# Latent attention as one sequence of steps, and row maxima turned four columns at once

## The chip, the core and the metric

The kernel runs on one core of one Trainium2 chip. Times are microseconds of device time of that core for one execution; smaller is better. A core has five engines that run their own instruction lists in order and meet through semaphores: TensorE (PE in the profile, with its weight loads as PEld), VectorE (DVE), ScalarE (ACT), GpSimd (POOL), and SyncE (SP), which here issues all DMAs. TensorE writes only to PSUM, which has eight banks of 512 fp32 columns by 128 partitions.

## The reference

One decoder layer over 2048 positions of width 1024. A norm and one input projection feed two groups of heads; their gated outputs go through one output projection, a gated per-layer embedding and a final norm. The change touches the second group only, eight latent heads with 96-wide queries and keys (64 made from a latent, 32 rotary and shared) and 64-wide values, under a causal mask:

```python
def mla_attention(q_nope, q_rope, k_nope, k_rope, v):
    scale = (MLA_NOPE + MLA_ROPE) ** -0.5
    sc = (einsum('bqhd,bkhd->bhqk', qn, k_nope) + einsum('bqhr,bkr->bhqk', qr, k_rope)) * scale
    pr = causal_probs(sc, start, s)          # softmax over the keys up to the query
    return einsum('bhqk,bkhd->bqhd', pr.astype(v.dtype), v)
```

## The kernel before

Four stages follow one another: projections, latent attention, differential attention, output. The latent stage works in *pairs of heads* `pr` (0 to 3) and *tiles of 512 queries* `t` (0 to 3). One head of a pair, `e`, in one tile is called a *run* here; the 32 runs come in the order pr, t, e and are numbered 0 to 31, and the two runs of one pr and t are called a *pair of runs*. A run has n = 4(t+1) steps, one for each block of 128 keys, up to the diagonal; on the last four the query columns left of the diagonal are left out, so they are 512, 384, 256 and 128 wide.

A step has two halves. `scores` makes 128 keys by 512 queries in PSUM with three matmuls of split numbers (lines 583 to 585, and 587 for the mask on the diagonal), exponentiates twice on ACT (588 rounded to `ph`, 589 in full), takes the rest `pl` on DVE (590), and adds `ph` to `acc` on POOL (596, 599) for most steps. The PSUM tile `pst` of a step is held from line 583 to line 590. `av`, three steps later (LAG), multiplies both parts with the values into `po` and `po2` (613, 614, and 616 where TensorE adds the softmax sum). A run ends with `finish`: line 620 adds the column sums of `acc` into `po2`, ACT and DVE put the output together in `ot` (622 to 624), four transposes turn it into `pz` (627), DVE divides (629, 631) and SP stores (633).

Each pair of runs needs a preparation, `prep`: queries and keys (lines 505 to 518), values for even pairs (533 to 535), and for each run the row maxima. `rmax` multiplies 128 queries with 512 keys (547, 549 on the diagonal) and DVE reduces them to a column (550). `row` then gathers the maxima of 512 queries in four columns `m4`, turns them with four transposes into one row of 512 in PSUM (560), and ACT writes the negative of it as row 96 of the queries `QH` (561). The first matmul of `scores` uses 97 rows, the 97th being this one, so a run's first score waits for its row.

PSUM tiles of the latent stage: `ps_m` (2 banks) for all preparation, `ps_s` (4 banks) for `pst`, `ps_o` for `po` and for `po2`, which `pz` shares.

The order is planned in Python. `main` holds the steps of all runs with a cost in TensorE and DVE time, `side` the preparation with its costs. Going backwards through `main`, the planner places side work as late as an even load of DVE allows (RHO, SLACK), and at least MARGIN = 13 entries of `main` ahead of the run that needs it; then the recorded instructions are ordered once more by a list scheduler that has its own estimate of durations and fills waits with whatever is ready. So the order on each engine isn't the order of the code. Before, `main` has each run's steps, its last three `av` alone, and its `finish`, before the next run begins:

```python
            for e in range(2):
                for kc in range(n + LAG):
                    if kc < n:
                        tasks[e].append((0.65 * w, 0.6 * w, lambda e=e, kc=kc: scores(e, kc)))
                    if kc >= LAG:
                        tasks[e].append((0.43 * w, 0, lambda e=e, kc=kc: av(e, kc - LAG)))
                tasks[e].append((1.2, 1.7, lambda e=e: finish(e)))
```

Of the kernel before, what the change touches and what calls it, by code (L numbers as in the profile page):

```python
# [7 lines left out]
F32 = mybir.dt.float32  # L8
# [9 lines left out]
P = 128  # L18
# [13 lines left out]
MARGIN = 13  # attention steps by which a latent head's preparation runs ahead  # L32
RHO = 0.95  # share of the tensor engine's time in which the vector engine may be busy
SLACK = 0.8  # vector work that may pile up
QB = 2  # buffers for a latent head's queries
HE = 6  # steps over which a differential head's loads are spread
WN = 6  # pieces of the output weights loaded in a step
PES = 4  # key blocks whose softmax sums are added by the tensor engine: those with
PEL = (3,)  # kc % PES in PEL
TAIL = 2  # in the last latent step, every TAIL-th of the other sums goes to the vector engine  # L40


def merge(a, b):
    """Runs two lists of (cost, function) side by side, each in its order."""
# [15 lines left out]
def tile_hymba(ctx, tc, a, out):  # L60
# [48 lines left out]
    with ExitStack() as c1:  # L109
# [136 lines left out]
        # gates of the differential heads  # L246
# [23 lines left out]
        # rotary q and k of the differential heads, transposed  # L270
# [28 lines left out]
        # shared rotary key and first gates of the latent heads  # L299
# [31 lines left out]
        # latents and the rotary part of the latent heads' q  # L331
# [100 lines left out]
    def load_head(h):  # L432
        """Queries, keys and values of a differential head, a tile for every 512 positions."""
# [21 lines left out]
    SC_M = 96.0 ** -0.5  # L455
    with ExitStack() as c2:
# [3 lines left out]
        ps_s = c2.enter_context(tc.tile_pool(name="p2pss", bufs=4, space=PSUM, reuse_waits="tile"))  # L460
# [35 lines left out]
        def prep(pr, t):  # L496
            """Keys, queries, values and row maxima of a pair of heads for one tile of 512 positions."""
# [43 lines left out]
            def rmax(e, j, c):  # L541
# [5 lines left out]
                T.matmul(pm[:, :w], lhsT=q, rhs=keys_of(pr, e, c)[0][0:96, :w], start=True, stop=(c < t))  # L547
# [473 lines left out]
```

## Time and profile before

| | us |
|---|---|
| median of 3 runs | 2062.68 (2057.31 to 2063.65) |
| span of the profiled execution | 2063.1 |
| latent stage within it | about 614 to 1199 |
| TensorE busy | 1958.6 (95%) |
| VectorE busy | 1268.7 (61%) |
| ScalarE busy | 934.4 (45%) |
| GpSimd busy | 465.7 (23%) |
| mean granted TensorE clock | 0.986 |

The profiled execution's time is its span, with nothing recorded around it. Shares of busy time are averages over stages with different limits. A matmul's recorded duration overlaps that of the next one, so what one costs is read from the distance between two starts. From the rows of the latent stage a reader should take, pair by pair, how long it lasted and how much of that TensorE and VectorE had work for.

### The profile page before, as it was taken

The page shows a single profiled execution, that of the slowest core. Times are in us where ns is not written, and L with a number is a line of the kernel's source. Part 1 is how long each engine was busy: PE and PEld are TensorE (multiplying, and loading weights), DVE is VectorE, ACT ScalarE, POOL GpSimd, SP SyncE. Part 2 cuts the span into 40 slices and gives each one's busy share as a digit, 9 for nine tenths or more (in the row PEclk, how much of TensorE's full clock was granted, in tenths as well). Part 3 has the DMA queues.
Part 4 walks back from the last instruction along what each step waited for, and adds up shares of the span by engine and source line. Part 5 has one row for each costly group of instructions (what it writes and reads, how often), then busy time and mean ns, then how long its engine had stood idle before and what let it go on. Part 6 is the DMA issues. An engine that isn't in the chain of part 4 may idle for free.

```text
span 2063.1 us, 28013 instructions
## 1 busy us (share of the span) xinstructions
PE 1958.6 (95%) x9793; PEld 1532.6 (74%) x9793; DVE 1268.7 (61%) x2714; ACT 934.4 (45%) x2105; POOL 465.7 (23%) x428
## 2 busy tenths in 40 slices
PE   8999999999989999999999988998898899999997
PEld 5788878898866776766767766776676677777786
DVE  5253676522457878878878887778888533333332
ACT  5422001123336675766666776778687321111111
POOL 4400445200002453534534410000001201111000
PEclk9999999999999999999999999999999999999999
DMA  5442333322120000000032240433011622222210
GB/s 166 136 155 96 124 131 123 113 86 71 42 75 14 16 11 21 14 16 16 11 90 78 59 118 9 128 105 90 6 57 57 230 77 87 87 87 84 78 46 21
DMA packets 126861, 156.20 MB, mean 76 GB/s; under 512 B 30385, under 2 KB 74305, under 8 KB 126721
## 3 DMA queue, kind: packets, MB, share of 16 engines
q1 hardware_dynamic: 126720, 154.42, 24.1%
q8 instruction: 77, 1.26, 0.3%
q14 instruction: 64, 0.52, 0.1%
HBM read 101.41 MB, written 52.96 MB: 75 GB/s over the span
## 4 chain that ended last, share of the span: by engine, by line
PE 75%; DVE 9%; ACT 7%; DMA 2%; issue 2%; POOL 1%; SPq 0%; ACTq 0%; POOLq 0%; DVEq 0%
PE p L914 6%; PE p L916 6%; PE p L915 6%; PE ps L165 5%; PE ps L166 5%; PE ps L164 5%; PE pm L547 3%; PE pod L815 3%; PE pst L583 3%; PE pst L584 3%; PE pst L585 3%; PE po L613 3%; PE po L614 3%; PE ps L284 3%; PE ps L283 3%; PE ps L282 3%
## 5 line engine op out<-in xcount | busy, mean ns | idle before, releaser
L599 POOL TENSOR_TENSOR acc<-ph,acc 128x512 f32<-128x512 f32 (+3 forms) x208 | 218.9, 1052 | 248.1 <-ACT ph L588 161.1
L164 PE MATMUL ps<-wh,xh 128*128 128x512 f32 (+1 forms) x640 | 229.2, 359 | 9.8 <-DVE wh L153 8.4
L165 PE MATMUL ps<-wl,xh 128*128 128x512 f32 (+1 forms) x640 | 227.3, 356 | 0.5 <-DVE wl L154 0.4
L166 PE MATMUL ps<-wh,xl 128*128 128x512 f32 (+1 forms) x640 | 226.3, 356 | 0.3 <-DVE xl L141 0.2
L588 ACT ACTIVATE ph<-pst 128x512 fp32r<-128x512 f32 (+1 forms) x320 | 170.8, 534 | 110.8 <-PE pst L585 66.5
L550 DVE TENSOR_REDUCE mx<-pm 128x1 f32<-128x512 f32 (+2 forms) x320 | 186.6, 605 | 28.6 <-PE pm L547 15.9
L590 DVE TENSOR_TENSOR pl<-pst,ph 128x512 fp32r<-128x512 f32 (+1 forms) x320 | 189.5, 604 | 22.8 <-ACT pst L589 21.2
L751 DVE TENSOR_REDUCE mxd<-pu 128x1 f32<-128x1024 f32 (+4 forms) x192 | 172.8, 909 | 22.7 <-PE pu L750 14.5
L99 POOL TENSOR_TENSOR s<-s,half 128x2 f32<-128x2 f32 (+1 forms) x48 | 32.1, 669 | 649.5 <-DVE s L98 549.6
L762 ACT ACTIVATE pb<-pu,nm 128x1024 f32<-128x1024 f32 (+4 forms) x192 | 165.4, 867 | 24.0 <-DVE nm L757 16.0
L589 ACT ACTIVATE pst<-pst 128x512 f32<-128x512 f32 (+1 forms) x320 | 170.1, 532 | 0.3
L747 PE MATMUL pu<-hd 128*128 128x512 f32 (+3 forms) x320 | 140.7, 440 | 20.4 <-ACT pb L762 19.3
L164 PEld LDWEIGHTS ps<-wh,xh 128*128 128x128 f32 x640 | 121.2, 190 | 29.9 <-ACT sq L136 6.5
L815 PE MATMUL pod<-ah,hd 128*128 128x256 f32 (+1 forms) x576 | 141.8, 371 | 0.5 <-ACT ah L807 0.5
L166 PEld LDWEIGHTS ps<-wh,xl 128*128 128x128 f32 x640 | 121.0, 189 | 19.4 <-DVE xl L141 2.2
L165 PEld LDWEIGHTS ps<-wl,xh 128*128 128x128 f32 x640 | 121.3, 190 | 18.7 <-DVE wl L154 1.9
L963 DVE TENSOR_TENSOR sg<-p,sg 128x512 f32<-128x512 f32 (+1 forms) x34 | 20.8, 655 | 171.5 <-ACT sg L962 171.5
L748 PE MATMUL pu<-hd 128*128 128x512 f32 (+3 forms) x320 | 122.1, 387 | 0.0
L547 PE MATMUL pm<-kall,QH 96*128 96x512 f32 (+3 forms) x288 | 112.2, 403 | 6.9 <-DVE kall L103 4.8
L613 PE MATMUL po<-ph,vall 128*128 128x512 f32 (+1 forms) x320 | 117.1, 394 | 0.5 <-ACT ph L588 0.2
L614 PE MATMUL po<-pl,vall 128*65 128x512 f32 (+1 forms) x320 | 111.9, 371 | 3.7 <-DVE pl L590 2.1
L583 PE MATMUL pst<-QH,kall 97*128 97x512 f32 (+3 forms) x288 | 114.0, 396 | 0.0
(266 smaller groups left out, 4654.1 us busy)
## 6 DMA issues: line engine op xcount, KB each, us to landing
hd<-dq_s SPq DMA_DIRECT2D x192, 128.0 KB, 2.7
wr<-in_w_in SPq DMA_DIRECT2D x40, 256.0 KB, 3.0
xr<-in_xT SPq DMA_DIRECT2D x32, 256.0 KB, 3.7
dq_s<-th SPq DMA_DIRECT2D x32, 256.0 KB, 2.0
dq_s<-tl SPq DMA_DIRECT2D x32, 256.0 KB, 2.0
xr<-in_x SPq DMA_DIRECT2D x16, 512.0 KB, 4.2
gt<-gate_s SPq DMA_DIRECT2D x15, 512.0 KB, 3.4
out<-sg SPq DMA_DIRECT2D x15, 512.0 KB, 2.9
```

What stands on the lines that cost most here:

```text
L164: T.matmul(pt[:, :w], lhsT=h, rhs=wh[k][:, :w], start=(k == 0), stop=False)
L165: T.matmul(pt[:, :w], lhsT=h, rhs=wl[k][:, :w], start=False, stop=False)
L166: T.matmul(pt[:, :w], lhsT=l, rhs=wh[k][:, :w], start=False, stop=(k == KT - 1))
L547: T.matmul(pm[:, :w], lhsT=q, rhs=keys_of(pr, e, c)[0][0:96, :w], start=True, stop=(c < t))
L550: V.reduce_max(box[e][:, j, c:c + 1], pm[:, :w], axis=AX.X)
L583: T.matmul(pt[:, o:], lhsT=kh[0:97], rhs=qh[0:97, o:], start=True, stop=False)
L590: V.tensor_sub(pl[:, o:], pt[:, o:], ph[:, o:].bitcast(F32))
L599: eng.tensor_add(box[e][:, o:], ph[:, o:].bitcast(F32), box[e][:, o:])
L613: T.matmul(po[:, o:], lhsT=vv[:, 0:128], rhs=ph[:, o:], start=(kc == 0), stop=(kc == n - 1))
L614: T.matmul(po2[:65, o:], lhsT=vv[:, 64:129], rhs=pl[:, o:], start=(kc == 0), stop=False)
L751: V.reduce_max(st["x", m][:, u:u + 1], pu[:, :w], axis=AX.X)
L815: T.matmul(st["po"][:, o:], lhsT=vv, rhs=st[u][:, i, o:], start=(kc == 0), stop=(kc == nk - 1))
```

## The change

Line numbers from here on are of the kernel they belong to; after the change scores are lines 593 to 597, `av` 618 to 621, the end of a run 624 to 639, and the turning of the row 558 to 562.

*Rows.* One transpose turns the four columns of `m4` at once into 4 partitions by 128 columns. ACT writes the negative of that into an SBUF tile `mr` (4 by 128), and four DMAs on SP put its four rows into row 96 of `QH`, 512 bytes each (the DMA is cut into 16 pieces of 8 numbers). Where t = 0, `m4` is a view of the maxima and the DVE copy is gone.

*One sequence.* A class `Run` replaces `attend`, and `stream` lists the steps of all 32 runs in one sequence: the first scores of a run stand directly behind the last scores of the run before, and its last three `av` between them. `finish` is cut in two: `gather` after the last `av`, and `store` three steps later. The costs the planner is told are a little higher (0.7 and 0.47 for 0.65 and 0.43; 0.9 and 0.4 on TensorE for 1.2).

*PSUM.* `ps_s` has 3 banks for 4, `po` has 2 for 1, and `pz` takes a bank of `ps_m`, not that of `po2`.

Everything else in the diff removes comments.

```diff
-        ps_s = c2.enter_context(tc.tile_pool(name="p2pss", bufs=4, space=PSUM, reuse_waits="tile"))
+        ps_s = c2.enter_context(tc.tile_pool(name="p2pss", bufs=3, space=PSUM, reuse_waits="tile"))
...
             def row(e):
-                m4 = sb.tile([P, 4], F32, name="m4", tag="m4")
+                m4 = box[e][:, :, 0]
                 if t > 0:
+                    m4 = sb.tile([P, 4], F32, name="m4", tag="m4")
                     V.reduce_max(m4, box[e][:, :, :t + 1], axis=AX.X)
-                else:
-                    V.tensor_copy(m4, box[e][:, :, 0])
-                prow = ps_m.tile([P, 512], F32, name="prow", tag="m")
+                pm = ps_m.tile([P, 512], F32, name="pm4", tag="m")
+                T.transpose(pm[:4, :P], m4, ident)
+                mr = sb.tile([4, P], F32R, name="mr", tag="mr", bufs=4)
+                A.mul(mr, pm[:4, :P], -1.0)
                 for j in range(4):
-                    T.transpose(prow[0:1, j * P:(j + 1) * P], m4[:, j:j + 1], ident)
-                A.mul(QH[pr, t, e][96:97, :], prow[0:1, :], -1.0)
+                    nc.sync.dma_start(out=QH[pr, t, e][96:97, j * P:(j + 1) * P].bitcast(F32),
+                                      in_=mr[j:j + 1, :].bitcast(F32))
...
-                    box["o", e] = (ps_o.tile([P, 512], F32, name="po", tag="po"),
-                                   ps_o.tile([P, 512], F32, name="po2", tag="po2"))
+                    self.po = ps_o.tile([P, 512], F32, name="po", tag="po", bufs=2)
+                    self.po2 = ps_o.tile([P, 512], F32, name="po2", tag="po2")
...
-            def finish(e):
-                po, po2 = box["o", e]
-                T.matmul(po2[:65], lhsT=sel, rhs=box[e], start=False, stop=True)
-                ot = sb.tile([P, 512], F32, name="ot", tag="ot", bufs=1)
...
-                pz = ps_o.tile([P, 4, P], F32, name="pz", tag="po2")
+            def gather(self):
+                T.matmul(self.po2[:65], lhsT=sel, rhs=self.acc, start=False, stop=True)
+                ot = self.ot = sb.tile([P, 512], F32, name="ot", tag="ot", bufs=1)
+                A.copy(ot[:65], self.po2[:65])
+                V.tensor_add(ot[0:64], self.po[0:64], ot[0:64])
+                V.tensor_add(ot[0:64], self.po[64:128], ot[0:64])
+
+            def store(self):
+                pz = ps_m.tile([P, 4, P], F32, name="pz", tag="m")
                 for j in range(4):
-                    T.transpose(pz[:, j, 0:65], ot[0:65, j * P:(j + 1) * P], ident[0:65, 0:65])
+                    T.transpose(pz[:, j, 0:65], self.ot[0:65, j * P:(j + 1) * P], ident[0:65, 0:65])
...
+        def stream(runs):
+            LAG, DROP = 3, 3
+            seq = [(r, kc) for r in runs for kc in range(r.n)]
+            main, start, late = [], [], {}
+            for i in range(len(seq) + LAG + DROP):
+                if i < len(seq):
+                    r, kc = seq[i]
+                    w = 1 - r.where(kc)[2] / 512
+                    if kc == 0:
+                        start.append(len(main))
+                    main.append((0.7 * w, 0.6 * w, lambda r=r, kc=kc: r.scores(kc)))
+                if LAG <= i < len(seq) + LAG:
+                    r, kc = seq[i - LAG]
+                    w = 1 - r.where(kc)[2] / 512
+                    main.append((0.47 * w, 0, lambda r=r, kc=kc: r.av(kc)))
+                    if kc == r.n - 1:
+                        main.append((0.9, 1.4, r.gather))
+                        late[i + DROP] = r
+                if i in late:
+                    main.append((0.4, 0.6, late[i].store))
+            assert len(late) == len(runs)
+            return main, start
```

Three places in the new order matter below. The first is SP's list early in the stage, of the kernel before: `QH` and `QL` are the rotary rows of a run's queries, loaded two pairs of runs ahead, and `zm_s` the outputs stored.

```order
L526 DMA QH<-qr_s_95 32x512
L527 DMA QL<-qr_s_95 32x512
L526 DMA QH<-qr_s_96 32x512
L527 DMA QL<-qr_s_96 32x512 x2
L526 DMA QH<-qr_s_96 32x512
L633 DMA zm_s_106<-zt 128x4x64 x2
L527 DMA QL<-qr_s_97 32x512
```

The same place after it, where line 562 is the row's DMAs (those of runs 0 and 1 first, then of 2 and 3).

```order
L562 DMA QH<-mr 1x16x8 x8
L527 DMA QL<-qr_s_96 32x512
L526 DMA QH<-qr_s_96 32x512
L562 DMA QH<-mr 1x16x8 x4
L527 DMA QL<-qr_s_96 32x512
L526 DMA QH<-qr_s_96 32x512
L562 DMA QH<-mr 1x16x8 x4
L639 DMA zm_s_106<-zt 128x4x64
```

The row's DMAs stand in the one list of SP, four to a run, between loads that wait for a buffer and stores that wait for a result; 128 of them are new.

The second place is TensorE's list at the last seam, from run 30 to run 31, before the change: the turning of run 31's row (560) and its first score (583, with the keys `kalt`).

```order
L613 MATMUL po<-ph,vall_5442 128x128 [waits Activation_49]
L614 MATMUL po_11615<-pl,vall_5442 65x512 [waits DVE_49]
L560 MATMUL prow<-ident,m_11772 1x128 [waits DVE_49]
L560 MATMUL prow<-ident,m_11772 1x128 x3
L614 MATMUL po_11615<-pl,vall_5442 65x384 [waits DVE_49]
L583 MATMUL pst<-QH,kalt 128x512 [waits Activation_49]
L614 MATMUL po_11615<-pl,vall_5442 65x256 [waits DVE_49]
L614 MATMUL po_11615<-pl,vall_5442 65x128 [waits DVE_49]
L620 MATMUL po_11615<-acc,sel 65x512 [waits DVE_49]
L584 MATMUL pst<-QL,kalt 128x512 [waits DMAHW5_49]
```

After it, the same seam from the last `av` of run 30 on; the turning of run 31's row (558) now stands 26 rows ahead of its first score (593).

```order
L618 MATMUL po<-ph,vall_5442 128x256 [waits Activation_49]
L619 MATMUL po_11663<-pl,vall_5442 65x256 [waits DVE_49]
L618 MATMUL po<-ph,vall_5442 128x128 [waits Activation_49]
L619 MATMUL po_11663<-pl,vall_5442 65x128 [waits DVE_49]
L624 MATMUL po_11663<-acc,sel 65x512 [waits Pool_49]
L593 MATMUL pst<-QH,kalt 128x512 [waits DMAHW6_49,DMAHW1_49,DMAHW7_49,DMAHW0_49,PE_49]
L594 MATMUL pst<-QL,kalt 128x512
L595 MATMUL pst<-QH,kalt 128x512
```

The first score of a run now waits for DMAs where it waited for ACT, and the scheduler has put TensorE work between the two: by the lists, a run's row is turned a few microseconds of TensorE work before its first score.

The third place is the end of the stage. Before, line 747 (the first matmul of the differential stage, on `pu`) stands ahead of the last run's transposes (627):

```order
L620 MATMUL po_11910<-acc,sel 65x512 [waits Pool_49]
L747 MATMUL pu<-hd 128x128
L748 MATMUL pu<-hd 128x128
L750 LDWEIGHTS ident_b
L750 MATMUL pu<-mask_b,ident_b 128x128
L747 MATMUL pu<-hd 128x128 [waits PE_49]
```

After it, where these lines are 765 to 768 and 633:

```order
L624 MATMUL po_11950<-acc,sel 65x512 [waits Pool_49]
L633 MATMUL pz<-ident,ot 128x65 [waits DVE_49,Activation_49]
L633 MATMUL pz<-ident,ot 128x65 x3
L765 MATMUL pu<-hd 128x128 [waits DVE_49,PE_49]
L766 MATMUL pu<-hd 128x128
```

`pz` lies now in a bank that the first `pu` also takes, so three blocks of the differential stage that stood ahead of the last transposes have moved behind them, and behind the DVE instruction that reads `pz`.

The planner's side work has moved too. Counted in TensorE's lists from the first score of one pair of runs to that of the next, the row maxima (line 547) stand like this, in the order of the pairs:

| pairs of runs with | maxima before | maxima after |
|---|---|---|
| t = 0 (4 pairs) | 12, 12, 12, 12 | 12, 16, 16, 15 |
| t = 1 | 26, 24, 26, 24 | 17, 15, 17, 16 |
| t = 2 | 22, 23, 22, 23 | 28, 27, 28, 27 |
| t = 3 | 22, 19, 22, 15 | 23, 18, 23, 14 |

The other 4 before, and 8 after, stand ahead of the first score.

## Rows read from the trace of the kernel before

**Rows 1.** The page: busy time by engine; the chain that ended last.

```profile
PE 1958.6 (95%) x9793; PEld 1532.6 (74%) x9793; DVE 1268.7 (61%) x2714; ACT 934.4 (45%) x2105; POOL 465.7 (23%) x428
PE 75%; DVE 9%; ACT 7%; DMA 2%; issue 2%; POOL 1%; SPq 0%; ACTq 0%; POOLq 0%; DVEq 0%
```

**Rows 2.** Windows, pairs with t = 0 or 1: length, busy by engine, clock.

```profile
core 0: us, PE busy (x) PEld busy (x) DVE busy (x) ACT busy (x) POOL busy (x), PEclk, DMA share, GB/s
641.90:677.20 35.30, 33.71 (x179) 23.70 (x178) 30.93 (x64) 21.44 (x47) 14.09 (x15) 1.00 0.08 19
...
sum 218.80, PE 207.04 PEld 146.44 DVE 183.59 ACT 125.53 POOL 66.69; mean PE 25.88 PEld 18.30 DVE 22.95 ACT 15.69 POOL 8.34
```

**Rows 3.** Windows, pairs with t = 2 or 3.

```profile
677.20:719.30 42.10, 41.58 (x211) 30.23 (x211) 34.67 (x66) 28.78 (x60) 20.10 (x18) 1.00 0.06 13
...
sum 360.20, PE 355.02 PEld 258.29 DVE 285.57 ACT 256.47 POOL 183.61; mean PE 44.38 PEld 32.29 DVE 35.70 ACT 32.06 POOL 22.95
```

**Rows 4.** Timeline at a turned row: start us, us, what, count, idle before.

```profile
640.16 0.60 PE L560 MATMUL prow<-ident,m 128*1 128x128 f32 x4 [1.04 <-DVE m L555]
640.80 0.59 ACT L561 ACTIVATE QH<-prow 1x512 fp32r<-1x512 f32 x1 [3.59 <-PE prow L560]
641.89 0.39 PE L583 MATMUL pst<-QH,kall 97*128 97x512 f32 x1
642.12 0.39 PE L584 MATMUL pst<-QL,kall 96*128 96x512 f32 x1
```

**Rows 5.** Waits, latent stage: us in total, times, longest.

```profile
PEld pv L533 <- ACT QH L561: 3.1, 7, 0.7
```

**Rows 6.** Groups by form, whole span: busy us, mean ns, idle before.

```profile
L590 DVE TENSOR_TENSOR pl<-pst,ph 128x512 fp32r<-128x512 f32 x224 | 152.0, 684 | 20.2 <-ACT pst L589 18.6
L550 DVE TENSOR_REDUCE mx<-pm 128x1 f32<-128x512 f32 x224 | 150.6, 686 | 21.0 <-PE pm L547 15.9 <-PE pm L549 2.4
L588 ACT ACTIVATE ph<-pst 128x512 fp32r<-128x512 f32 x224 | 133.9, 598 | 85.3 <-PE pst L585 66.5 <-PE pst L587 9.3 <-issue 4.4
L589 ACT ACTIVATE pst<-pst 128x512 f32<-128x512 f32 x224 | 133.4, 595 | 0.2
L588 ACT ACTIVATE ph<-pst 128x128 fp32r<-128x128 f32 x32 | 8.9, 279 | 17.0 <-PE pst L587 10.6 <-POOL acc L599 6.4
```

**Rows 7.** Timeline of SP's DMA issues.

```profile
611.36 0.41 SPq L527 DMA_DIRECT2D QL<-qr_s  x1
611.82 0.41 SPq L526 DMA_DIRECT2D QH<-qr_s  x1
```

**Rows 8.** DMA issues, latent stage: KB each, median us to landing.

```profile
zm_s<-zt SPq DMA_DIRECT2D x32, 128.0 KB, 1.9
QL<-qr_s SPq DMA_DIRECT2D x32, 64.0 KB, 1.8
```

**Rows 9.** Timeline at the end of the latent stage.

```profile
1195.21 1.02 PE L620 MATMUL po<-acc,sel 128*65 128x512 f32 x2
1195.67 0.62 PE L747 MATMUL pu<-hd 128*128 128x128 f32 x1
1196.27 0.58 ACT L622 COPY ot<-po 65x512 f32<-65x512 f32 x1 [1.65 <-PE po L620]
1196.89 0.68 DVE L623 TENSOR_TENSOR ot<-po,ot 64x512 f32<-64x512 f32 x1
1197.86 0.69 DVE L624 TENSOR_TENSOR ot<-po,ot 64x512 f32<-64x512 f32 x1
1198.70 0.43 PE L627 MATMUL pz<-ident,ot 65*128 65x65 f32 x4 [1.56 <-DVE nm L759]
1199.39 0.42 DVE L631 TENSOR_TENSOR zt<-pz,rs 128x256 f32<-128x256 f32 x1
```

**Rows 10.** Windows around a fall of the clock.

```profile
774.70:784.90 10.20, 8.93 (x49) 6.20 (x47) 8.40 (x17) 5.80 (x13) 0.31 (x1) 1.00 0.09 22
784.90:795.10 10.20, 10.13 (x31) 6.67 (x32) 7.41 (x18) 2.91 (x6) 3.51 (x4) 0.50 0.06 14
```

More of the change, by code (lines that the diff above doesn't have):

```diff
@@ L546, in rmax @@
                 pm = ps_m.tile([P, 512], F32, name="pm", tag="m")
-                T.matmul(pm[:, :w], lhsT=q, rhs=keys_of(pr, e, c)[0][0:96, :w], start=True, stop=(c < t))
+                T.matmul(pm[:, :w], lhsT=q, rhs=keys_of(pr, e, c)[0][0:96, :w], start=True, stop=c < t)
                 if c == t:
@@ L566, in prep, with __init__, by_pe, where @@
             return [(1.95, 1.3, queries), (0.65, 1.3, keys)], val, maxes
-        def attend(pr, t):
-            tasks = [[], []]
-            n = 4 * (t + 1)
-            box = {}
-            def scores(e, kc):
+        class Run:
+            def __init__(self, pr, t, e):
+                self.pr, self.t, self.e, self.n = pr, t, e, 4 * (t + 1)
+                self.p = {}
+            def by_pe(self, kc):
+                return kc >= 2 and kc < 4 * self.t and kc % PES in PEL
+            def where(self, kc):
+                c, j = kc // 4, kc % 4
+                return c, j, j * P if c == self.t else 0
+            def scores(self, kc):
+                pr, t, e = self.pr, self.t, self.e
                 qh, ql = QH[pr, t, e], QL[pr, t, e]
@@ L578, in scores @@
                 pl = s3.tile([P, 512], F32R, name="pl", tag="pl")
-                box[e, kc] = ph, pl
-                c, j = kc // 4, kc % 4
-                o = j * P if c == t else 0
+                self.p[kc] = ph, pl
+                c, j, o = self.where(kc)
                 kh, kl = (x[:, j * P:(j + 1) * P] for x in keys_of(pr, e, c))
@@ new lines, in av @@
+                    self.po2 = ps_o.tile([P, 512], F32, name="po2", tag="po2")
+                ph, pl = self.p.pop(kc)
+                c, j, o = self.where(kc)
+                vv = vt[c][:, j, 2 * (self.pr % 2) + self.e]
+                T.matmul(self.po[:, o:], lhsT=vv[:, 0:128], rhs=ph[:, o:], start=(kc == 0), stop=(kc == self.n - 1))
+                T.matmul(self.po2[:65, o:], lhsT=vv[:, 64:129], rhs=pl[:, o:], start=(kc == 0), stop=False)
+                if self.by_pe(kc):
+                    T.matmul(self.po2[:65, o:], lhsT=selh, rhs=ph[:, o:], start=False, stop=False)
@@ L631, in finish @@
                 V.tensor_mul(zt, pz[:, :, 0:64], rs.broadcast_to([P, 4, 64]))
-                h0 = (2 * pr + e) * 64
-                nc.sync.dma_start(out=zm_s[t][:, h0:h0 + 64].rearrange("(j p) d -> p j d", p=P), in_=zt)
-            LAG = 3
-            for e in range(2):
-                for kc in range(n + LAG):
-                    w = 1 if kc // 4 < t else 1 - (kc % 4) / 4
-                    if kc < n:
-                        tasks[e].append((0.65 * w, 0.6 * w, lambda e=e, kc=kc: scores(e, kc)))
-                    if kc >= LAG:
-                        tasks[e].append((0.43 * w, 0, lambda e=e, kc=kc: av(e, kc - LAG)))
-                tasks[e].append((1.2, 1.7, lambda e=e: finish(e)))
-            return tasks
+                h0 = (2 * self.pr + self.e) * 64
+                nc.sync.dma_start(out=zm_s[self.t][:, h0:h0 + 64].rearrange("(j p) d -> p j d", p=P), in_=zt)
+        def stream(runs):
[20 more added lines that the diff above has]
+            return main, start
         steps = [(pr, t) for pr in range(4) for t in range(NT)]
-        main, side, start = [], [], {}
+        main, start = stream([Run(pr, t, e) for pr, t in steps for e in range(2)])
+        side = []
         for i, (pr, t) in enumerate(steps):
@@ L655, in tile_hymba @@
             side += [(2 * i + 1, 2 * (i - t), x) for x in second]
-            for e, tasks in enumerate(attend(pr, t)):
-                start[2 * i + e] = len(main)
-                main += tasks
         place = [0] * len(side)
```

26 lines of the change are left out of this document (6 added, 20 removed).

## The prediction

> **What bounds the kernel now.** I read the page's busy times and chain first, then windows cut at the first score of each pair of runs, then the timeline inside them, the waits, the groups and the DMA issues. The reader should see in [rows 1] that TensorE is busy 95% of the span and makes 75% of the chain, with VectorE (9%) and ScalarE (7%) behind it: a change pays here by giving TensorE less to do or by closing its gaps, and little else counts.
>
> Where the gaps of the latent stage are, the windows tell. Recorded matmuls overlap, so I count them at their pitch: two 512-column passes start 0.23 us apart (641.89 and 642.12 in [rows 4]), narrower ones in proportion. At this pitch the matmuls of the eight short pairs (t = 0 and 1) make about 175 us of the 218.8 in [rows 2]; 44 are lost, half of them in the four pairs with t = 1. The eight long pairs need about 338 of 360.2 [rows 3] and lose 22. In the t = 1 window of [rows 2] VectorE is busy 30.93 of 35.30 us, 88%; in the t = 2 window of [rows 3] 34.67 of 42.10, 82%. So VectorE nearly sets the pace in the short pairs, because the maxima for the long runs are reduced there. A second loss is the clock: at 784.9 the granted clock falls to 0.50 (1.2 of 2.4 GHz) for 10.2 us, and 31 matmuls run where 49 ran before [rows 10]. In the stretch ahead of it TensorE was busy 8.93 of 10.2 us. There are three such stretches in the stage, two in its middle, at a pair with t = 0 or 1, each worth about 4 us.
>
> **The change part by part.**
>
> *Fewer transposes.* Four turn a row in 0.60 us [rows 4]; a matmul's record outlasts its pitch by 0.39 − 0.23 = 0.16, so four cost 0.44, one 0.11. Three of four go in each of 32 runs: 96 × 0.11 = −10.5 us, on the engine that sets the end. If they stood only in gaps it would be nothing.
>
> *Row maxima spread.* By the new lists 35 maxima leave the t = 1 pairs and 20 come into the t = 2 pairs. One costs VectorE 0.69 us [rows 6] and TensorE 0.23. If VectorE sets the pace in both places, 35 × (0.69 − 0.23) = −16 comes from the first, of the 22 lost there, and 20 × 0.46 = +9 to the second. VectorE in a t = 2 pair would go from 82% to (34.67 + 5 × 0.69)/42.1 = 90%, and in a t = 1 pair from 88% to about 83%. I take both, −7; the ends are −16 and +9.
>
> *The row's slot and ACT.* Seven times TensorE's loads waited, 3.1 us together, for ACT to have read the PSUM row [rows 5]. ACT now reads 128 columns, 0.28 for 0.59 us [rows 6, 4], and the bank is free sooner: −2, between −3.1 and 0.
>
> *Clock.* A t = 1 pair with fewer gaps may keep the full clock. Of −8 (both middle stretches) and 0 I take −3. I leave +4 (a new stretch) to the range.
>
> *The row's DMAs.* Before, a row was ready 0.60 + 0.04 + 0.59 = 1.25 us after its first transpose began [rows 4]. After, I add one transpose 0.27 (0.60 less three pitches), 0.04, ACT 0.28, some 0.1 to SP, and on SP four issues, the last starting 3 × 0.46 = 1.38 us after the first [rows 7]. The trace shows no DMA of 32-byte pieces from SBUF to SBUF. Nearest are the loads `QL` (1.8 us from issue to landing) and the stores `zm_s` (1.9) [rows 8], the latter in pieces of 256 bytes; I take 1.9. Together 4.0 us. The page "DMA: Bandwidth & Descriptors" of the Trainium skill (section Specifications) says that pieces under 512 bytes are read, changed and written back; by that these DMAs would land later than `QL`. Its piece is 2048 bytes and 0.1 us faster than `zm_s`, which shows no such price for 256. What the rule would do to the time is the third rival below.
>
> In TensorE's new list I counted the work between the row's transpose and the run's first score, at the pitches above: 17 of 32 runs have less than 4.0 us, 2.2 the least, and the shortfalls add up to 10.5 us. Behind a waiting first score stands all of TensorE's list, since it is in order; ACT and VectorE run dry one step later. Part of it falls into time that TensorE loses anyway (a first score often waits for VectorE's maxima); I take half, +5. Ends: 0, where the scheduler's order drifts in favour, and +21, where the chain takes 4.6 us. The 128 issues take SP 128 × 0.46 = 59 us of a 585 us stage, and `zm_s` and the loads for two pairs later queue behind a row that waits for ACT; with SP nearly idle I give that nothing.
>
> *Three `pst` tiles.* A full-width tile is held from its first matmul to line 590: 0.46 for two passes and 0.39 for the third [rows 4], ACT 0.60 and 0.60, VectorE 0.68 [rows 6], with a little between them, 2.8 us at the least. Three tiles allow one step per 0.93 us. A step of TensorE is five passes, 1.15 us, plus preparation. In the last run, with nothing else to do, 16 steps have to pass at that pace; VectorE's maxima of 0.69 each, in front of line 590, can hold a tile 0.7 longer, 3.5 in all and 1.17 a step, just over TensorE's pace. I take +3; ends 0 and 224 full-width steps × 0.1 = +22. The second `po` bank lets a run's first `av` start before the last run's output is added; the seams are few and overlapped before, so I take nothing for it.
>
> *End of the stage.* In [rows 9] three blocks of `pu` stand ahead of the transposes, while ACT (0.58) and VectorE (0.68 and 0.69) make `ot`, and TensorE idles 1.56 us. After, transposes 0.43, reciprocal and line 631 (0.42) stand ahead of the first `pu`, which loses its cover: +3, between 1 and 4.
>
> *Joining the runs.* That the first scores of a run stand directly behind the last of the previous one brings nothing more: the scheduler had already put run 31's first score among run 30's last `av`.
>
> Sum: −10.5 − 7 − 2 − 3 + 5 + 3 + 3 = −11.5. The profiled execution took 2063.1 us and lies 0.4 above the median: 2051.6, so 2052. Taken together, likely errors of the terms give 2042 to 2060 for this case. About 0.3%, 6.2 us, is what a measurement of this kernel can tell from no change: faster means under 2056.5, slower over 2068.9.
>
> **Rivals.**
>
> *More is gained.* The t = 1 pairs give their whole −16, nothing comes back at t = 2, both clock stretches go (−8), three tiles suffice: −10.5 − 16 − 2 − 8 + 5 + 3 = −28.5, 2035 us. For it: [rows 10] shows the clock falling right after a thin stretch. Against: t = 2 is at 82% already.
>
> *The gain is eaten.* Maxima moved bring nothing, since the list scheduler fills gaps either way, the clock stays, and rows come late in full: −10.5 − 2 + 10.5 + 3 + 3 = +4, 2067 us. For it: the half I took off the DMA shortfall is a choice. Against: the t = 1 pairs do have 22 us to give.
>
> *Slower, by late rows.* If a row DMA lands in 3.0 us, the chain takes 5.1 and the shortfalls add up to 31 us: 2052 + 31 − 5 = 2078. It decides from a landing of about 2.6 us up (4.65 us of chain, 22 us in all). For it: pieces of 32 bytes, below every one in [rows 8]. Against: 512 bytes in all, and landings there of 64 and 128 KB differ by 0.1 only.
>
> *Slower, by three tiles.* If each of the 224 full-width steps [rows 6] waits 0.1 us for its tile, 22 instead of 3: 2071. It decides from 0.09 us a step. For it: the fourth tile covers just such a VectorE delay. Against: the planner and the scheduler know the three banks, and the new order leaves a tile a median of 3.8 us of TensorE work (count times pitch) before it is used again.
>
> **How the numbers follow.** The forecast 2052 has 0.42, more gained 0.17, the gain eaten 0.25, late rows 0.09, three tiles 0.07. Faster: 0.37 of the forecast's share, all 0.17, and 0.02 of the eaten gain: 0.56. Slower: 0.05 of the eaten gain, 0.07 and 0.05 of the last two: 0.17. The rest, 0.27, is no change. The range 2035 to 2070 leaves out half of the gain case below and most of both slower cases above.
>
> **What would show it.** In the profile after: 32 transposes at line 558, 0.27 us each, for 128. First scores (line 593) that wait for a DMA, in total about 5 us; over 20 would be the third rival, under 1 the upper case. Row DMAs landing in 1.8 to 2.0 us. Windows of the t = 1 pairs shorter by some 4 us each, t = 2 pairs longer by about 2; if t = 1 pairs stay, my reading that VectorE sets their pace is wrong. Fewer half-clock stretches between 780 and 1090. First matmuls of a step waiting for line 600's `pl` would speak for the fourth rival. Line 765 starting some 3 us after line 624's end, where before line 747 followed line 620 at once. The forecast fails if the sum over the short pairs does not fall by 10 us or more, or if the waits of the row exceed what the transposes save.

## The result and the profile after

| | before | after |
|---|---|---|
| median, us | 2062.07 (2057.31 to 2063.65, 4 runs) | 2081.29 (2079.36 to 2082.92, 4 runs) |
| ratio, 95% interval | | 1.0095 (1.0082 to 1.0109) |
| span of the profiled execution | 2063.1 | 2077.6 |
| mean granted clock | 0.986 | 0.981 |

The kernel became 0.95% slower, 19 us; 2052 was forecast. Of all timed runs told of here one, of slots4_onedma_first, took 2698 us at a granted clock of 0.65; its kernel's median and ratio leave it out. The page's busy line and chain, to be read against [rows 1]:

```profile
PE 1964.4 (95%) x9697; PEld 1533.5 (74%) x9697; DVE 1273.1 (61%) x2706; ACT 924.4 (44%) x2105; POOL 465.6 (22%) x428
PE 74%; DVE 8%; ACT 7%; DMA 3%; issue 2%; POOL 1%; SPq 1%; ACTq 0%; POOLq 0%; DVEq 0%
```

96 matmuls fewer, and TensorE is busy 5.8 us longer. The windows, cut at the same events (columns as in [rows 2]): first and sum of the eight short pairs, then two and the sum of the eight long ones.

```profile
625.00:651.90 26.90, 23.08 (x91) 16.36 (x91) 15.00 (x31) 11.64 (x26) 3.97 (x5) 0.70 0.04 9
651.90:683.10 31.20, 29.89 (x160) 21.85 (x159) 26.83 (x55) 20.27 (x45) 12.28 (x12) 1.00 0.07 17
...
sum 212.80, PE 199.93 PEld 139.88 DVE 169.82 ACT 118.20 POOL 65.82; mean PE 24.99 PEld 17.48 DVE 21.23 ACT 14.78 POOL 8.23
```

```profile
683.10:725.40 42.30, 41.24 (x205) 29.98 (x204) 37.28 (x71) 28.58 (x62) 20.02 (x18) 1.00 0.05 12
...
1020.80:1075.00 54.20, 53.33 (x258) 38.57 (x257) 40.33 (x73) 36.81 (x77) 28.30 (x25) 1.00 0.16 42
...
sum 374.90, PE 362.05 PEld 261.41 DVE 298.51 ACT 252.91 POOL 184.24; mean PE 45.26 PEld 32.68 DVE 37.31 ACT 31.61 POOL 23.03
```

The 14.5 us between the two profiled spans divide as follows. The stage's first score stands at 625.0, before at 620.8: +4.2 (counted from the stage's first row maximum it comes after 10.0 us, before after 6.3: 3.7 later). The short pairs take 212.8 for 218.8: −6.0. The long ones 374.9 for 360.2: +14.7. What follows, +1.6. Among the short pairs the four with t = 1 are 12 us shorter (126.3 for 138.1), and those with t = 0 are 6 us longer. Of the long ones the t = 2 pairs are 4 us longer and the t = 3 pairs, of which the forecast says nothing, 10.6. So where maxima left, the pairs got shorter, as forecast; something else took more.

Counting matmuls at their pitch again, from the first score of the stage to that of the last pair, TensorE has some 12 us less to do. It loses some 12 more in waits at full clock and 6 more to half clock. The waits have a name. Waits of the latent stage (us, times, longest), after:

```profile
PEld pst L593 <- DVE pl L600: 13.9, 21, 1.5
PEld po L618 <- ACT ph L598: 10.6, 29, 1.5
PE pst L593 <- DVE pl L600: 8.4, 14, 1.4
PE po L618 <- ACT ph L598: 3.5, 10, 1.4
PE pst L593 <- DMA QH<-mr: 1.0, 4, 0.3
```

First matmuls of a step wait for line 600, which frees a `pst` tile: the fourth rival's sign, hardly there before (0.5 us). The rows of PEld and PE must not be added: a weight load and the matmul behind it stand idle in the same time. With the overlap counted once the two rows cover 14.2 us, and TensorE's matmuls themselves waited 8.4. For a row's DMA a first score waits 1 us in all.

The clock is best seen in one window over the whole stage. Before, then after:

```profile
605.00:1215.00 610.00, 584.59 (x2915) 421.05 (x2914) 490.00 (x971) 396.14 (x839) 251.00 (x233) 0.97 0.14 39
```

```profile
605.00:1215.00 610.00, 577.10 (x2751) 412.08 (x2749) 479.86 (x923) 376.75 (x808) 250.06 (x232) 0.95 0.13 35
```

By the clock's own records that is 37.5 us at half clock before and 58.0 after (records that reach into the window are counted whole here and below; 55.1 of the 58.0 lie inside it). In [rows 10] TensorE does 49 matmuls in 8.93 busy us at full clock and 31 in 10.13 at half (0.50, 1.2 of 2.4 GHz), so a microsecond at half clock costs about 0.45, an estimate: some 9 us.

The profiled pair shows the clock's part too small. Each timed run has its mean clock on record: the four after have 0.979 to 0.981, and the profiled one is one of them; but the 84 timed runs of the kernel before in the experiments below have 0.984 to 0.993, 0.989 on the median, and the profiled one of before only 0.986. At half clock the mean loses half of that time, so 0.980 for 0.989 is some 37 us more at half clock in the whole kernel. A straight line through those 84 runs gives 0.32 us of time for each microsecond at half clock, less than the 0.45. By these two prices, estimates both, the clock makes 12 to 17 of the 19 us.

Much of it lies at the start: 27 us at half clock from 613.7 on, before 10 from 614.2 on. Four windows of 10 us after the change:

```profile
614.00:624.00 10.00, 7.71 (x26) 5.59 (x26) 5.56 (x14) 2.34 (x6) 0.00 (x0) 0.50 0.05 14
624.00:634.00 10.00, 8.70 (x29) 6.17 (x28) 2.87 (x5) 3.29 (x5) 0.00 (x0) 0.66 0.01 1
634.00:644.00 10.00, 8.41 (x27) 5.08 (x27) 7.33 (x14) 4.54 (x12) 2.21 (x3) 0.68 0.05 13
644.00:654.00 10.00, 9.07 (x47) 7.26 (x48) 7.66 (x19) 5.33 (x14) 2.22 (x3) 0.81 0.05 14
```

In the same windows before, the clock is 0.51, 0.98, 1.00 and 1.00; this is the second of them:

```profile
624.00:634.00 10.00, 9.62 (x52) 6.70 (x50) 6.78 (x15) 7.57 (x16) 2.22 (x3) 0.98 0.04 13
```

The timeline shows what is there, the first row on its way:

```profile
618.49 0.38 PE L558 MATMUL pm<-ident,mx 128*4 128x128 f32 x1 [0.78 <-DVE mx L550]
618.90 0.27 ACT L560 ACTIVATE mr<-pm 4x128 fp32r<-4x128 f32 x1 [4.22 <-PE pm L558]
619.19 2.51 SPq L562 DMA_DIRECT2D QH<-mr  x4
625.00 0.78 PE L593 MATMUL pst<-QH,kall 97*128 97x512 f32 x1
```

Four issues take 2.51 us, then the last must land; 6.5 us after the transpose the first score starts. It doesn't wait there for the DMA by the profile: the scheduler has put values and the second run's maxima ahead of it. Until it starts, ACT and VectorE have no scores to work on: in the window from 624 ACT is busy 3.3 us for 7.6 before. That this is why TensorE is thin afterwards too is likely, not shown.

The DMA issues (KB, median us to landing), beside the loads and stores of the same stage:

```profile
zm_s<-zt SPq DMA_DIRECT2D x32, 128.0 KB, 1.9
QL<-qr_s SPq DMA_DIRECT2D x32, 64.0 KB, 1.9
QH<-mr SPq DMA_DIRECT2D x128, 0.5 KB, 1.7
```

### The profile page after: what moved, and what is told of

Read it like the earlier page. It is cut to its first block, busy times and chain, and to the rows that moved or that the text cites. A ratio compares the mean times of both kernels' runs of the same rounds, so it can differ in the third digit from the quotient of the medians.

```text
span 2077.6 us, 28044 instructions
## 1 busy us (share of the span) xinstructions
PE 1964.4 (95%) x9697; PEld 1533.5 (74%) x9697; DVE 1273.1 (61%) x2706; ACT 924.4 (44%) x2105; POOL 465.6 (22%) x428
## 4 chain that ended last, share of the span: by engine, by line
PE 74%; DVE 8%; ACT 7%; DMA 3%; issue 2%; POOL 1%; SPq 1%; ACTq 0%; POOLq 0%; DVEq 0%
PE p L932 6%; PE p L934 6%; PE p L933 6%; PE ps L165 5%; PE ps L166 5%; PE ps L164 5%; PE pm L547 3%; PE pod L833 3%; PE pst L593 3%; PE pst L595 3%; PE pst L594 3%; PE ps L284 3%; PE ps L283 3%; PE ps L282 3%; PE po L618 3%; PE po L619 2%
## 5 line engine op out<-in xcount | busy, mean ns | idle before, releaser
L547 PE MATMUL pm<-kall,QH 96*128 96x512 f32 (+3 forms) x288 | 116.7, 420 | 8.7 <-DVE kall L103 4.4
L619 PE MATMUL po<-pl,vall 128*65 128x512 f32 (+1 forms) x320 | 117.2, 374 | 0.2
```

## The experiments

Names that begin with b_ are the kernel before with an edit, the others the changed kernel with one. Times are medians, with the ratio to the kernel before on the same chip. The last column is the mean granted clock of the timed runs, median and range; microseconds at half clock within the stage are from the one profiled execution of each. The kernel before had medians of 2059.2 to 2062.1 us in the different rounds, so two edited kernels of different rounds compare better by their ratios than by their times.

| kernel | us | ratio (95%) | granted clock |
|---|---|---|---|
| before (84 runs) | | | 0.989 (0.984 to 0.993) |
| after | 2081.3 | 1.0095 (1.0082 to 1.0109) | 0.980 (0.979 to 0.981) |
| slots4 | 2071.7 | 1.0055 (1.0039 to 1.0070) | 0.981 (0.979 to 0.983) |
| oldrow | 2067.9 | 1.0034 (1.0022 to 1.0045) | 0.988 (0.987 to 0.989) |
| slots4_oldrow | 2069.5 | 1.0045 (1.0026 to 1.0064) | 0.988 (0.984 to 0.990) |
| after_4t | 2077.6 | 1.0086 (1.0069 to 1.0104) | 0.988 (0.986 to 0.989) |
| after_first | 2071.5 | 1.0054 (1.0039 to 1.0069) | 0.984 (0.982 to 0.986) |
| after_costs | 2077.6 | 1.0082 (1.0062 to 1.0103) | 0.980 (0.978 to 0.983) |
| after_onedma | 2064.4 | 1.0016 (1.0003 to 1.0028) | 0.985 (0.982 to 0.989) |
| slots4_onedma | 2067.6 | 1.0036 (1.0025 to 1.0047) | 0.981 (0.980 to 0.985) |
| after_onedma_first | 2059.9 | 1.0002 (0.9987 to 1.0017) | 0.986 (0.982 to 0.988) |
| slots4_onedma_first | 2064.6 | 1.0024 (1.0012 to 1.0035) | 0.982 (0.980 to 0.984) |
| b_slots3 | 2089.3 | 1.0142 (1.0122 to 1.0161) | 0.983 (0.978 to 0.984) |
| b_newrow | 2071.2 | 1.0046 (1.0031 to 1.0061) | 0.981 (0.979 to 0.982) |
| b_newrow_m17 | 2064.9 | 1.0020 (1.0010 to 1.0030) | 0.982 (0.981 to 0.983) |
| b_costs | 2064.5 | 1.0016 (1.0006 to 1.0025) | 0.990 (0.986 to 0.992) |
| b_rowdma | 2073.4 | 1.0072 (1.0047 to 1.0097) | 0.984 (0.981 to 0.985) |
| b_onet | 2059.0 | 0.9997 (0.9987 to 1.0006) | 0.984 (0.981 to 0.986) |
| b_onedma | 2052.8 | 0.9965 (0.9952 to 0.9978) | 0.984 (0.983 to 0.985) |
| b_onedma_first | 2050.7 | 0.9951 (0.9935 to 0.9967) | 0.987 (0.986 to 0.989) |

### The parts, undone or done alone

**slots4**

```diff
-p2pss bufs=3        +p2pss bufs=4
-po bufs=2           +po bufs=1
```

> The changed kernel with four pst tiles again and one po bank for two (8 banks in all). Theory A, three pst tiles are too few: first matmuls of a step waited 22 us for the pl that frees a tile; with four tiles this goes, and the time is about 2058 to 2064. Theory B, the row's DMAs are late: nothing here touches them, about 2080. Theory C, the new place of the work (start of the stage and its half-clock stretches) costs the time: about 2075 to 2082.

2071.7: half of the loss. The waits for a tile go, as its waits show:

```profile
PE pst L593 <- DMA QH<-mr: 4.2, 9, 1.2
PEld po L618 <- ACT ph L598: 3.4, 6, 1.1
PE po L618 <- ACT ph L598: 1.7, 3, 1.0
PEld pst L593 <- DVE pl L600: 1.4, 3, 0.9
```

Theory A took the 22 us from the two rows added, 13.9 and 8.4, which overlap. Of the 8.4 us that the matmuls themselves waited for line 600, 0.6 are left, and 9.6 us came back: about the true wait, half of what theory A asked.

**oldrow**

```diff
-one transpose, mr, four DMAs
+four transposes, A.mul(QH[pr, t, e][96:97, :], prow[0:1, :], -1.0)
```

> The changed kernel with the row turned as before (four transposes, ACT writes row 96, no DMA). Theory A: the 96 transposes come back on TensorE, 2081 + 10 = about 2090, less if some stand in waits. Theory B: the wait for the DMAs goes, about 2065. Theory C: near 2080 to 2090.

2067.9, near theory B: the row's new way is a cost, 13 us, though it saves 96 transposes. The clock goes from 0.980 to 0.988.

**b_slots3**

```diff
-p2pss bufs=4        +p2pss bufs=3
```

> The kernel before with three pst tiles for four, one bank left unused, nothing else. Theory A: 2062 + 15 to 20 = about 2080. Theory B and C: within 5 us of 2062.

2089.3, more than theory A asked. In the old sequence three tiles cost 28 us, with the same two signs and a clock of 0.983 for 0.989:

```profile
PEld po L613 <- ACT ph L588: 12.7, 34, 0.7
PEld pst L583 <- DVE pl L590: 4.5, 13, 0.8
PE po L613 <- ACT ph L588: 2.4, 10, 0.4
PE pst L583 <- DVE pl L590: 1.7, 5, 0.6
```

**b_newrow**

```diff
-four transposes, A.mul into QH
+one transpose, mr, four DMAs
```

> The kernel before with the row alone turned in the new way (one transpose, ACT, four DMAs). Theory A: 96 transposes less on TensorE, some 10 us faster if the DMAs are in time, about 2053 to 2058. Theory B: slower than before, 2070 or more. Theory C: near 2055 to 2062.

2071.2: theory B by the number. But the first scores wait 2.4 us in all for a row's DMA. The first score of the stage stands 10.0 us after the stage's first row maximum, before 6.3. Counted as above, work for TensorE falls by 10 us and its waits at full clock grow by 7; the clock of the timed runs is 0.981 for 0.989.

**slots4_oldrow**

```diff
 slots4 and oldrow together
```

> The changed kernel with four pst tiles and one po bank and with the row turned as before: what is left of the change is the joined sequence, the store three steps later, pz in the preparation's banks, and the planner's costs. If the two parts add up (10 from three tiles, 13 from the row), 2081 - 23 = 2058, a little faster than before; if the joined sequence itself costs time, 2063 to 2068.

2069.5. The two gains don't add up; what is left of the change (the joined sequence, `pz`, the costs) is itself slower than the kernel before by 0.45%, at nearly the same clock (0.988). With the old row a fourth tile gives nothing (2067.9 without it).

### Are the transposes worth their time?

**b_onet**

```diff
-for j in range(4): T.transpose(prow[0:1, j * P:(j + 1) * P], m4[:, j:j + 1], ident)
-A.mul(QH[pr, t, e][96:97, :], prow[0:1, :], -1.0)
+T.transpose(prow[0:4, 0], m4, ident)
+A.mul(QH[96:97] as (1, 4, P), prow[0:1, 0:1].broadcast_to([1, 4, P]), -1.0)
```

> The kernel before with one transpose for four and no DMA: ACT writes the first quarter's maxima into all four quarters of row 96, so three quarters of the rows hold the wrong maxima, and the exponents are scaled by 0.02 so that nothing overflows; the work is else the same. Theory T1, the 96 transposes are on the path and worth their 10 us: 2051. Theory T2, they stand in time that TensorE loses anyway, since VectorE sets the pace where they are: 2058 to 2062.

0.9997, the number of theory T2: 96 transposes taken away without any DMA bring no time. But T2's reason, that they stand in time which TensorE loses anyway, isn't what the runs show. The ten timed runs have a mean clock of 0.984 on the median, the sixteen of the kernel before in the same round 0.989: some 20 us more at half clock, 7 to 9 us of time by the two prices. At the same clock the transposes are worth something: at 0.984 to 0.986 b_onet took 2057.9 to 2060.3 (eight runs), the kernel before 2064.1 to 2065.7 (four, in all rounds). The two profiled executions have the same clock, before and then b_onet, and lie 7.0 us apart:

```profile
core 0: 2063.1 us, clock 0.986
```

```profile
core 0: 2056.1 us, clock 0.986
```

So 5 to 7 us of the 10 are there, and the lower clock takes them back. (b_onet also puts smaller numbers through the exponentials; after_4t, next, changes no number that is used.)

**after_4t**

```diff
-T.transpose(pm[:4, :P], m4, ident)
+for j in (3, 2, 1, 0): T.transpose(pm[:4, j * P:(j + 1) * P], m4, ident)
```

> The changed kernel with three idle transposes more in each row (the same columns into other parts of the same PSUM tile, read by nobody): the 96 transposes are back on TensorE, the DMAs stay. If the transposes were worth their 10 us, 2081 + 10 = 2091. If they stood in time that TensorE loses anyway, or kept the clock up, 2076 to 2084.

2077.6: with 96 transposes more it isn't slower, which rules out the 2091; that it is 3.7 us faster isn't shown, as its ratio (1.0086) lies within the interval of the changed kernel's. Its four timed runs have a clock of 0.986 to 0.989, the changed kernel's 0.979 to 0.981. Over the stage the profile has 0.98 for 0.95, by the records 27.3 us at half clock for 58.0:

```profile
605.00:1215.00 610.00, 576.74 (x2845) 411.49 (x2845) 480.33 (x923) 375.86 (x803) 249.98 (x232) 0.98 0.13 35
```

So in this kernel too what the transposes saved was about what the lower clock took.

### The row's way over DMAs

**b_rowdma**

```diff
-A.mul(QH[pr, t, e][96:97, :], prow[0:1, :], -1.0)
+A.mul(mr, prow[0:1, :], -1.0); one DMA of 2 KB from mr to QH[96:97]
```

> The kernel before with its four transposes, ACT writing the row of 512 to an SBUF tile, and one DMA of 2 KB from there to row 96. No transposes saved, the way over a DMA added. The row in four DMAs with the transposes saved cost 10 us. T1: the saving of 10 is missing, 2061 + 20 = about 2080. T2: about 2071 or a little less, as only one DMA is issued.

2073.4, nearer to T2's 2071 than to T1's 2080, and 14 us over the kernel before.

**b_onedma**

```diff
-four DMAs, a row of mr each
+one DMA, QH[96:97] as (1, 4, P) from mr
```

> The kernel before with the new row, but one DMA of four rows for the four DMAs. T1 and T2: the chain is three issues (3 x 0.58 = 1.7 us) shorter for each row. If the chain's length counts in most of the 32 runs, 2071 falls by 10 or more, to 2055 to 2061; if it counts at the first run alone, to 2069.

2052.8, faster than before. One issue for four gave 18 us. The least time from a row's transpose to its run's first score is 2.7 us here; with four DMAs it is 4.2 or more in all 32 runs. With four, waits for the DMA itself were 2.4 us, so the gain isn't these waits alone: the clock goes from 0.981 to 0.984, and a shorter chain may let the scheduler put less ahead of the first scores, which isn't shown. b_rowdma, also with a single DMA and at the same clock, is 20 us slower than this; the transposes, 5 to 7 us at the same clock, are a part of that, and the rest no run explains. Nor does one explain why this is 6 us faster than b_onet, which saves the same transposes at the same clock without a DMA.

**after_onedma**

```diff
 the changed kernel, its four DMAs as one
```

> The changed kernel with one DMA of four rows for the four DMAs, three pst tiles as changed. If the four issues cost here what they cost in the kernel before (2071.2 to 2052.8, 18 us), 2081 - 18 = 2063. If they cost only at the first run, where the first score came 1.4 us later, 2078.

2064.4: 17 us back, as the first reading said, at a clock of 0.985 for 0.980. Where in the stage they come back, the number doesn't tell.

**after_first**

```diff
+if (pr, t) == (0, 0): four transposes, A.mul into QH; return
```

> The changed kernel with the rows of the first pair of runs alone turned as before, without DMAs (2 of 32 rows). If the start of the stage, where the first score came 3.7 us later and half clock lasted 27 us for 10, is a place of its own for the loss, the time falls by 6 to 11 us, to 2070 to 2075. If the four DMAs cost all along the stage, 2077 to 2081.

2071.5: two rows of 32 carry 10 us (8 by the ratios). The same four windows of its profile:

```profile
614.00:624.00 10.00, 9.32 (x34) 6.88 (x35) 4.89 (x11) 3.22 (x7) 0.00 (x0) 0.52 0.08 25
624.00:634.00 10.00, 9.66 (x53) 7.17 (x53) 7.61 (x16) 8.05 (x18) 2.22 (x3) 0.97 0.05 13
634.00:644.00 10.00, 8.43 (x47) 5.52 (x46) 9.04 (x20) 3.58 (x11) 2.22 (x3) 1.00 0.06 14
644.00:654.00 10.00, 9.77 (x45) 6.49 (x45) 7.16 (x13) 6.09 (x12) 2.60 (x2) 1.00 0.01 2
```

From 624 on it runs 53 matmuls where the changed kernel ran 29, with the clock at 0.97 for 0.66.

**after_onedma_first**

```diff
 after_onedma and after_first together
```

> The changed kernel with one DMA a row and the first pair's rows as before: of the row's way over DMA 30 single DMAs are left, the three pst tiles and the joined sequence stay. One DMA alone gave 17 us (2064), the first pair alone 10 (2071). If these are two costs that add up, 2081 - 17 - 10 + 1.4 (what one DMA already gave at the start) = about 2056; if they are one and the same, 2063 to 2066.

2059.9, between the two expectations: 21 us, not 27. The start is a part of what one DMA gives. That is the whole loss against the kernel before: with the row's chain short, the changed kernel is as fast. Against the old sequence with the same row (b_onedma_first, below) it is 9 us slower.

**b_newrow_m17**

```diff
-MARGIN = 13         +MARGIN = 17
```

> The kernel before with the new row (2071.2) and MARGIN 17 for 13, so that a run's preparation is due four steps earlier. If the loss comes from rows that are due too late for a chain of 4.2 us, the first scores get more lead and the time falls to 2060 or less. If it comes from work crowded ahead of the rows, it stays at 2067 to 2075.

2064.9, 6 us of 10 back, between the two: part of the loss was likely rows due too late for the longer chain, though a larger MARGIN moves all preparation, not the rows alone.

### Three tiles and the joined sequence

**slots4_onedma**

```diff
 after_onedma with slots4
```

> The changed kernel with four pst tiles, one po bank and one DMA of four rows. If what the row's DMAs and the third tile cost adds up, 2071.7 - 18 = 2053, as fast as the kernel before with one DMA. If the joined sequence costs by itself (with the old row and four tiles it was 2069.5), about 2060.

2067.6, a miss: no faster than with three tiles. The matmuls' waits for `pl` (line 599 in these two kernels) go from 4.6 us to 0.4, but the clock over the stage falls, first three tiles, then four:

```profile
605.00:1215.00 610.00, 576.74 (x2833) 414.86 (x2834) 494.34 (x970) 388.90 (x839) 251.06 (x233) 0.97 0.15 39
```

```profile
605.00:1215.00 610.00, 581.05 (x2774) 416.29 (x2775) 485.94 (x943) 379.22 (x820) 250.01 (x232) 0.95 0.14 37
```

By the records that is 37.5 us at half clock with three tiles and 64.9 with four, some 9 to 12 us. In the ten timed runs of each the clock is 0.985 and 0.981, some 17 us more at half clock, 5 to 7 us of time: more than the waits that went.

**slots4_onedma_first**

```diff
 slots4_onedma and after_first together
```

> The same with four pst tiles and one po bank: the joined sequence is left of what moved the time. If the joined sequence costs nothing by itself, about 2051, as the kernel before with the same row (2050.7); if it costs what it did with the old row (8 us) or with one DMA (15 us), 2059 to 2066.

2064.6, as if the joined sequence costs by itself; again slower than with three tiles (2059.9), at a clock of 0.982 for 0.986 in the timed runs.

**b_costs**

```diff
-0.65 and 0.43 a step, (1.2, 1.7) a run's end
+0.7 and 0.47 a step, (1.3, 2.0) a run's end
```

> The kernel before with the planner told the changed costs alone (0.7 and 0.47 for 0.65 and 0.43, and 1.3 and 2.0 for a run's end); no instruction is added or left out, only the order moves. If the costs the planner is told are a part of the loss of the joined sequence (8 us with four tiles and the old row), 2064 to 2070. If not, within 4 us of 2060.

2064.5: +0.16%, by the order alone; its clock is no lower than that of the kernel before (0.990).

**after_costs**

```diff
-0.7 and 0.47 a step, (0.9, 1.4) and (0.4, 0.6) a run's end
+0.65 and 0.43 a step, (0.8, 1.2) and (0.4, 0.5) a run's end
```

> The changed kernel with the planner told the costs of before (0.65 and 0.43 a step, 1.2 and 1.7 for a run's end). If the costs told are a part of the loss, 2081 falls by 3.5 us or more, as they added 3.5 to the kernel before; if the order's luck decides, it can move either way by some 5 us.

2077.6, 3.7 us less, but the ratios' intervals overlap (1.0062 to 1.0103 and 1.0082 to 1.0109): not told apart from no change, and no sign for either reading.

**b_onedma_first**

```diff
 b_onedma, the first pair's rows as before
```

> The kernel before with the new row in one DMA (2052.8), the rows of the first pair of runs turned as before. If the start is worth its 2.3 us and a half-clock stretch, 2047 to 2051; if not, 2052 to 2054.

2050.7, the fastest of all, 0.5% under the kernel before, at a clock of 0.987. It beats both kernels and is the version to keep.

## Why the prediction was wrong

Forecast 2052, range to 2070; measured 2081. Two steps failed: work taken off TensorE was counted as time gained at a clock that holds or rises, and a longer chain was priced by the wait it would show.

**Fewer transposes, −10.5: the gain was there, and the clock took it.** "On the engine that sets the end" was taken from a busy share of 95% in the profile [rows 1]. TensorE did get less work, some 12 us in the profile, and at the same clock the transposes are worth 5 to 7 us (b_onet). But where they went the clock fell, from 0.989 to 0.984 in b_onet, and where they came back it rose, from 0.980 to 0.988 in after_4t, and neither kernel's time moved clear of noise. It isn't so everywhere: b_onedma_first has 90 transposes fewer at 0.987 and gains 9 us, and what holds the clock up there no run shows. The prediction put the transposes and the clock in separate terms that have nothing to do with each other; half the gain of the forecast hung on the first.

**The row's DMAs, +5: mis-sized.** The chain was sized well: 4.0 us forecast, 4.1 the least from a row's transpose to its first score in the changed kernel; the landing 1.7 for 1.9. The four issues took 2.51 us where the prediction's step gave 4 × 0.46 = 1.84. What failed was to price a longer chain by the wait it would show. That wait is 1 us, and the price 17 (after_onedma), 21 with the first pair's rows (after_onedma_first). Of the 21 some 8 to 11 are the clock's, 0.980 for 0.986. The rest shows in other places: 3.7 us later for the first score of the stage, and waits of TensorE elsewhere; that they come from work put ahead of first scores is likely, not shown. The first pair of runs, with no scores of earlier runs to cover the chain, alone carried 8 to 10 us, and the prediction had no term for it.

**The clock, −3: wrong sign.** About +9 in the profiled pair, 12 to 17 in the timed runs; a part of it is also in the price of the DMAs above. I argued that a t = 1 pair with fewer gaps keeps the clock; three of those four pairs did run at full clock, but taking work off TensorE lowered the clock elsewhere. In the profile of the changed kernel the stretch in the third of the four, from 941.4, again follows a thin one:

```profile
931.40:941.40 10.00, 7.93 (x42) 5.10 (x41) 7.71 (x18) 3.53 (x11) 2.22 (x3) 1.00 0.06 13
941.40:955.10 13.70, 13.46 (x38) 9.78 (x37) 7.09 (x13) 5.40 (x11) 2.57 (x2) 0.50 0.05 10
```

**Three `pst` tiles, +3: too small.** TensorE's matmuls waited 8.4 us for a tile, between the forecast's 3 and the fourth rival's 22, and slots4 gave back 9.6. But with one DMA, or with the old row, four tiles gave nothing. The third tile's price is thus not a number of its own in the changed kernel; in the old sequence it is 28 us. slots4 also takes away one `po` bank, and no run separates the two.

**Row maxima spread, −7: right in place.** The t = 1 pairs lost 12 of the 16 forecast, three of the four 4 to 5 us each, while the one with the half-clock stretch grew by 2; the t = 2 pairs gained 4 of 9. The short pairs together fell by 6.0, short of the 10 that the prediction asked of itself, since the t = 0 pairs grew. The 10.6 us of the t = 3 pairs had no term; 5.2 of them are one pair with 18 matmuls more than before (1020.80 above, 258 for 240), and the short pair behind it has 28 fewer. No run moves the maxima alone.

**The row's slot and ACT, −2: about right.** Line 533's weight loads wait 0.6 us for ACT to have read the row, before 3.1.

**End of the stage, +3: nothing.** The timeline after shows the idle that was forecast:

```profile
1208.27 1.02 PE L624 MATMUL po<-acc,sel 128*65 128x512 f32 x2
1209.33 0.58 ACT L626 COPY ot<-po 65x512 f32<-65x512 f32 x1 [1.66 <-PE po L624]
1210.66 0.69 DVE L628 TENSOR_TENSOR ot<-po,ot 64x512 f32<-64x512 f32 x1
1211.50 0.43 PE L633 MATMUL pz<-ident,ot 65*128 65x65 f32 x4 [2.21 <-DVE ot L628]
1212.19 0.42 DVE L637 TENSOR_TENSOR zt<-pz,rs 128x256 f32<-128x256 f32 x1
1212.76 0.30 PE L765 MATMUL pu<-hd 128*128 128x128 f32 x1 [0.82 <-DVE zt L637]
```

Line 765 starts 4.5 us after line 624, before at once [rows 9]. But the hundredth matmul on `pu` starts 41.6 us after it in both kernels: something else sets the pace there, and the lost cover costs nothing.

**Joining the runs, 0: it costs.** With the same row (one DMA, the first pair as before) the old sequence takes 2050.7 and the joined one 2059.9 with three tiles and 2064.6 with four: 9 to 14 us. The 9 aren't the clock's, 0.987 and 0.986; of the other 5 the clock's fall to 0.982 can make all. A part may be the costs told to the planner (3.5 us in the old sequence). How the rest divides among the sequence, the later store and the banks stays open.

**The rivals.** Slower by late rows gave the right sign and nearly the time (2078), for a reason that didn't happen: on the median the row's DMAs landed no later than others of the stage, and first scores hardly waited. The Trainium skill's page "DMA: Bandwidth & Descriptors" (section Specifications) has pieces under 512 bytes read, changed and written back; these of 32 bytes landed in 1.7 us, `QL` in 1.9, so no price of it shows here. Slower by three tiles, 2071, had waits of the right kind, 8.4 us for its 22. "The gain is eaten" was right that the gain would go, but it took the clock as staying, and the clock is what ate most of it. No case had a lower clock with fewer transposes.

In one line, from the medians: 2060 before; −9 for the row in one DMA with the first pair as it was; +9 for the joined sequence with three tiles; +21 for four DMAs and the first pair's rows over them. It ends at 2081.

## What to carry to other kernels

On an engine that is 95% busy, work taken away is a gain only if nothing else is late in that stretch and its clock holds when it thins out: read the mean clock of every timed run beside its time, and compare kernels at the same clock before saying what a piece of work is worth. A longer chain ahead of a run's first instruction can cost far more than the wait that this instruction will show (17 us for 1 here), so price it at the place with no cover, the start, first, and by the time from its first instruction to its use. Don't add the waits of weight loads to those of their matmuls. Put several small DMAs of one tile into one, and read a change of 0.3% against what a mere change of the planner's costs does to the same kernel (0.16% here).

## What was not expected of the hardware

An issue on SP of a row's 512-byte DMA takes 0.58 us on the median (497 to 1638 ns over 128), more than the 0.41 of a load of 64 KB [rows 7]; one DMA of the same 2 KB in all lands in 1.6 us (b_rowdma), as soon as one of 0.5 KB. And the granted clock can make work cheap, both ways: 96 transposes more in after_4t came with a mean clock of 0.988 for 0.980 and no longer time, 96 fewer in b_onet with 0.984 for 0.989 and no shorter time.
